# First stage of w_in: the first scale wholly on TensorE in columns of 256, x first, half of g1 on TensorE, more background loads

## The chip, the core and the metric

The kernel runs on one core of a Trainium2 chip. The metric is the device time of one execution, in microseconds. Everything is one program: matmuls on TensorE (PE), elementwise work on VectorE (DVE) and ScalarE (ACT), and nearly all loads issued by SyncE (SP) in one queue, in program order.

## The reference

Two transformer blocks on x of 256 tokens by 2048 features, in float32. The change touches the first stage of the first block and the modulation vectors around it:

```python
c_act = silu(c)                                   # 2048
mod = c_act @ w_mod[l] + b_mod[l]                 # 2048 x 12288
sh1, sc1, g1, sh2, sc2, g2 = split(mod, 6)
h = rms_norm(x, norm_attn[l]) * (1.0 + sc1) + sh1
qa, ka, va, qb, ckv, qi, ki, wi = split(h @ w_in[l])
...                                               # two attentions
x = x + g1 * (mix @ w_out[l])
h = rms_norm(x, norm_ffn[l]) * (1.0 + sc2) + sh2
x = x + g2 * conv_ffn(h, w_up[l], conv_w[l], conv_b[l], w_down[l])
```

Then follow a second block with eight more vectors of the same kind (from `c_2`), a gated MLP mixer and a latent attention. Each of the 14 vectors is a product of one row of 2048 with a matrix of 2048 by 2048, 16.8 MB of weights to load for 2048 numbers.

## The kernel before

**Layout.** Activations lie with features on partitions: `X` is 16 tiles of 128 features by 256 tokens. A weight load brings 128 by 2048 float32 (1.05 MB) into one of `NRAW` = 5 buffers with the tag `raw`, used in turn; a load waits until the one five before it is done with. `parts` (L326) splits a load into a high and a low part: ScalarE rounds (L331), VectorE subtracts (L332). `product` (L335) makes three matmuls for each pair of tiles from them (L342 to L344).

**Modulation vectors.** There are two ways to make one. `mod_part` (L431) loads 128 columns, laid out as 128 by 2048, into a `raw` buffer (tile `mraw`), and VectorE multiplies it by silu(c) and adds up, 128 results in one instruction (L452). `mod_cols` (L457) does it on TensorE: a load holds four chunks of 128 rows by 512 columns; each chunk is the moving operand of a matmul whose stationary operand is a chunk of silu(c) in the first of 32 columns, and the four write to four strips of 32 partitions of one PSUM bank. After four loads the bank is copied (L469), four small matmuls with ones add the strips and turn the line into columns (L472), and VectorE adds the bias (L474): 512 results. `sc1` has its first half by `mod_cols` and its second by `mod_part`, `g1` is by `mod_cols` whole, all others are by `mod_part`.

**Order.** `setup` (L654) interleaves the first quarter of `sc1`, four columns of `sh1`, the load of x, the squares of x (ScalarE, L676, and matmuls with ones, L678) and the reciprocal root R, which a matmul with ones spreads into a row (L299). `first_attention` (L701) then multiplies `w_a` (qi, ckv, ka, va, ki, wi: 1616 columns, 13 output tiles in 7 PSUM banks) tile by tile: `modulated` makes the modulated tile k of x, `tile_of(k)` (L717) loads tile k of `w_a` (0.83 MB), splits it and makes 39 matmuls. The vectors for later tiles are made between the tiles; `tables` (L685) loads the tables of the attention and writes a bias to DRAM that SP issues (L699) behind a small product.

Then come 16 `query` blocks with the index scores, the top-k and the first attention's heads between them, the keys and values of the second, and `w_out` in two halves of 8 blocks with the second attention's heads in the first half. The feed-forward part begins with `opening` (L363), whose first products need the shift `sh2` as two more columns (`shifts`, L532) and the scaled x of all 16 tiles.

**Background.** `mod_rest` is a generator over all vectors behind `sh1`, in the order of use (g1, sc2, sh2, g2, ...); each step issues one load and its work. `step(rate)` (L488), called with every weight block, adds the rate to a credit and takes a step for each whole one. `need(name)` (L494) runs the generator until the vector is complete, however many steps that takes:

```python
RP, RWA, RWB, RF, RG, RM = 1.0, 2.0, 1.0, 0.82, 0.5, 0.6   # L43: queries, w_out 1, w_out 2, ...

    def need(self, name):
        while name not in self.mod or self.mod[name][1] < DB:
            next(self.bg)
        return self.mod[name][0]
```

So until the feed-forward part there are 16 x 1.0 + 8 x 2.0 + 8 x 1.0 = 40 steps, of which g1, sc2 and sh2 would take 48. The framework keeps each engine's instructions in an order that a scheduler makes from the program order and priorities; SP issues in order.

Of the kernel before, what the change touches and what calls it, by code (L numbers as in the profile page):

```python
# [42 lines left out]
RP, RWA, RWB, RF, RG, RM = 1.0, 2.0, 1.0, 0.82, 0.5, 0.6  # L43
# [20 lines left out]
def _layout(a):  # L64
# [12 lines left out]
    def at(m_, a_, k_):  # L77
# [6 lines left out]
    m["w_cols"] = c(np.stack([ws[n].reshape(4, 4, P, 4, 512).transpose(3, 0, 2, 1, 4) for n in COLS])  # L84
                    ).reshape(len(COLS), 4, 4, P, 2048)
# [117 lines left out]
class Build:  # L203
# [226 lines left out]

    def mod_part(self, name, j):  # L431

        i = MODS.index(name)
        src = "c_row" if i < 6 else "c2_row"
        if self.c_src != src:
            self.c_src = src
            self.c_all = self.wp.tile([P, D], F32, name="c_all", tag="c_all", bufs=1)
            if i < 6:
                self.nc.sync.dma_start(self.c_all[:1], self.ap[src])
                for q in range(4):  # L440
                    s = slice(q * 512, q * 512 + 512)
                    ps = self.bank()
                    self.nc.tensor.matmul(ps, self.ones[:1], self.c_all[:1, s], start=True, stop=True)
                    self.nc.scalar.activation(self.c_all[:, s], ps, AF.Silu)
            else:
                self.nc.sync.dma_start(self.c_all, self.ap[src].to_broadcast((P, D)))
                self.nc.scalar.activation(self.c_all, self.c_all, AF.Silu)
# [9 lines left out]
    def mod_cols(self, name, q):  # L457
# [10 lines left out]
        line = self.pair().rearrange("p a b -> p (a b)")  # L468
        nc.scalar.copy(line, bank)  # L469
        ps = self.bank()  # L470
        for b in range(4):
            nc.tensor.matmul(ps[:, b:b + 1], line[:, b * P:(b + 1) * P], self.ones[:, :1], start=True, stop=True)  # L472
        s = slice(4 * q, 4 * q + 4)
        nc.vector.tensor_add(self.mod_tile(name)[:, s], ps[:, :4], self.vec("b_" + name, 4 * q, 4))  # L474
        self.mod[name][1] += 4
# [886 lines left out]
```

## Time and profile before

| | |
|---|---|
| time, median of 3 runs (lowest to highest) | 2346.66 us (2345.24 to 2349.06) |
| the profiled execution: its time / its span | 2345.78 us / 2344.1 us |
| TensorE matmul busy / weight load busy | 2261.0 us (96%) / 2148.6 us (92%) |
| VectorE / ScalarE busy | 1826.3 us (78%) / 1155.0 us (49%) |
| mean granted clock of TensorE | 0.984 of full speed |
| moved by the DMAs | 629.59 MB, mean 269 GB/s |
| chain that ended last, by engine | TensorE 81%, VectorE 5%, ScalarE 1%, issue 1% |

Busy times are shares of the whole span and hide the stages: the sections of the program are bound by different things. A matmul's end is modelled, so a TensorE at 10.00 of 10 us need not run at its peak. A wait is put down to what released it last. The granted clock of a stretch is 1.00 at 2.4 GHz and 0.50 at 1.2 GHz, and a mean of the two in between.

### The profile page before, as it was taken

The page shows a single profiled execution, that of the slowest core. Times are in us where ns is not written, and L with a number is a line of the kernel's source. Part 1 is how long each engine was busy: PE and PEld are TensorE (multiplying, and loading weights), DVE is VectorE, ACT ScalarE, POOL GpSimd, SP SyncE. Part 2 cuts the span into 40 slices and gives each one's busy share as a digit, 9 for nine tenths or more (in the row PEclk, how much of TensorE's full clock was granted, in tenths as well). Part 3 has the DMA queues.
Part 4 walks back from the last instruction along what each step waited for, and adds up shares of the span by engine and source line. Part 5 has one row for each costly group of instructions (what it writes and reads, how often), then busy time and mean ns, then how long its engine had stood idle before and what let it go on. Part 6 is the DMA issues. An engine that isn't in the chain of part 4 may idle for free.

```text
span 2344.1 us, 42822 instructions
## 1 busy us (share of the span) xinstructions
PE 2261.0 (96%) x17578; PEld 2148.6 (92%) x17578; DVE 1826.3 (78%) x2989; ACT 1155.0 (49%) x1926; POOL 4.9 (0%) x8
## 2 busy tenths in 40 slices
PE   6879999699999999999999999999999999899999
PEld 4777888699999999999998889999999999899899
DVE  4777478999888888888889768877776568767785
ACT  2345666465444444444566444434444356555552
POOL 0000000000000000000000000000000000000000
PEclk9899999899999999999999999999999999999999
DMA  7987698989998899898767776877776555434342
GB/s 303 364 325 252 224 337 329 337 297 348 335 371 327 317 353 345 314 359 330 277 236 259 284 282 237 312 279 272 272 270 216 180 184 185 139 143 174 140 144 90
DMA packets 98053, 629.59 MB, mean 269 GB/s; under 512 B 10977, under 2 KB 18113, under 8 KB 30785
## 3 DMA queue, kind: packets, MB, share of 16 engines
q1 hardware_dynamic: 97858, 626.87, 73.2%
q8 instruction: 137, 2.24, 0.4%
q14 instruction: 58, 0.48, 0.1%
HBM read 624.68 MB, written 2.15 MB: 267 GB/s over the span
## 4 chain that ended last, share of the span: by engine, by line
PE 81%; DVE 5%; ACT 1%; issue 1%; ACTq 0%; DVEq 0%
PE bank L342 22%; PE bank L343 22%; PE bank L344 22%; PE bank L408 4%; PE bank L409 4%; PE bank L410 4%; DVE mraw L452 1%; DVE wl L332 1%; PE bank L1048 1%; DVE X L568 0%; PE bank L1245 0%; PE bank L595 0%; ACT wh L331 0%; PE bank L390 0%; PE bank L603 0%
## 5 line engine op out<-in xcount | busy, mean ns | idle before, releaser
L342 PE MATMUL bank<-act,wh 128*128 128x256 f32 (+1 forms) x4800 | 1360.9, 284 | 22.5 <-ACT act L539 21.0
L343 PE MATMUL bank<-act,wh 128*128 128x256 f32 x4800 | 1352.7, 282 | 0.7 <-DVE act L263 0.6
L344 PE MATMUL bank<-act,wl 128*128 128x256 f32 (+1 forms) x4800 | 1350.6, 281 | 0.0
L331 ACT ACTIVATE wh<-raw 128x1024 fp32r<-128x1024 f32 (+3 forms) x770 | 764.4, 1001 | 704.2 <-PE bank L343 493.4
L332 DVE TENSOR_TENSOR wl<-raw,wh 128x1024 fp32r<-128x1024 f32 (+3 forms) x770 | 879.0, 1152 | 247.8 <-ACT wh L331 245.8
L342 PEld LDWEIGHTS bank<-act,wh 128*128 128x128 f32 x4800 | 908.3, 189 | 36.7 <-ACT act L539 21.2
L343 PEld LDWEIGHTS bank<-act,wh 128*128 128x128 f32 x4800 | 909.2, 189 | 1.7 <-DVE act L263 1.3
L344 PEld LDWEIGHTS bank<-act,wl 128*128 128x128 f32 x4800 | 907.5, 189 | 0.1
L452 DVE CUSTOM_DVE_ANT_0 mraw<-mraw,c_all,k_vecs 128x2048 f32<-128x2048 f32 x200 | 469.1, 2348 | 44.2 <-DMA mraw<-in_wmods_dram 28.3
L408 PE MATMUL bank<-wh,act 128*128 128x512 f32 (+1 forms) x392 | 152.4, 389 | 0.0
L409 PE MATMUL bank<-wl,act 128*128 128x512 f32 (+1 forms) x392 | 151.5, 386 | 0.0
L410 PE MATMUL bank<-wh,act 128*128 128x512 f32 (+1 forms) x392 | 151.3, 386 | 0.0
L262 ACT ACTIVATE act<-t 128x256 fp32r<-128x256 f32 x166 | 66.9, 414 | 112.3 <-DVE t L945 68.1
L408 PEld LDWEIGHTS bank<-wh,act 128*128 128x128 f32 x392 | 73.7, 188 | 15.9 <-PE bank L1252 1.0
L410 PEld LDWEIGHTS bank<-wh,act 128*128 128x128 f32 x392 | 73.6, 188 | 15.4 <-issue 0.7
L409 PEld LDWEIGHTS bank<-wl,act 128*128 128x128 f32 x392 | 73.7, 188 | 15.0 <-issue 0.7
L728 PE MATMUL bank<-act,wh 128*128 128x256 f32 (+1 forms) x208 | 61.0, 304 | 26.9 <-ACT wh L331 26.8
L263 DVE TENSOR_TENSOR act<-t,act 128x256 fp32r<-128x256 f32 x166 | 68.2, 424 | 17.1 <-ACT act L262 16.3
L728 PEld LDWEIGHTS bank<-act,wh 128*128 128x128 f32 (+1 forms) x208 | 41.9, 203 | 32.1 <-ACT wh L331 30.5
L934 ACT ACTIVATE t<-bank,k_vecs 128x256 f32<-128x256 f32 x41 | 23.0, 561 | 93.2 <-PE bank L344 93.2
L729 PE MATMUL bank<-act,wh 128*128 128x256 f32 (+1 forms) x208 | 59.9, 298 | 0.0
L730 PE MATMUL bank<-act,wl 128*128 128x256 f32 (+1 forms) x208 | 56.7, 304 | 0.3 <-DVE wl L332 0.3
(235 smaller groups left out, 1415.3 us busy)
## 6 DMA issues: line engine op xcount, KB each, us to landing
mraw<-in_wmods_dram SPq DMA_DIRECT2D x200, 1024.0 KB, 6.4
raw<-in_w_up_dram SPq DMA_DIRECT2D x88, 1024.0 KB, 5.9
raw<-in_w_down_dram SPq DMA_DIRECT2D x64, 704.0 KB, 5.6
raw<-in_w_u_dram SPq DMA_DIRECT2D x32, 1024.0 KB, 5.0
raw<-in_w_v_dram SPq DMA_DIRECT2D x32, 1024.0 KB, 4.9
raw<-in_w_z_dram SPq DMA_DIRECT2D x32, 1024.0 KB, 4.9
raw<-in_w_ao_dram SPq DMA_DIRECT2D x32, 1024.0 KB, 4.8
raw<-in_w_cols_dram SPq DMA_DIRECT2D x24, 1024.0 KB, 5.6
```

Of the source, the lines that this page charges most:

```text
L262: self.nc.scalar.activation(hi, src, AF.Copy)
L263: self.nc.vector.tensor_sub(lo, src, hi.bitcast(F32))
L331: nc.scalar.activation(h[:, :n], raw[:, lo:hi], AF.Copy)
L332: nc.vector.tensor_sub(l[:, :n], raw[:, lo:hi], h[:, :n].bitcast(F32))
L342: mm(ps[:, :n], h[:, s], x[:, :n], start=first and k == 0, stop=False)
L343: mm(ps[:, :T], h[:, s], x[:, LO:], start=False, stop=False)
L344: mm(ps[:, :n], l[:, s], x[:, :n], start=False, stop=last and k == len(xs) - 1)
L408: mm(ps, xh, h[:, s], start=k == 0, stop=False)
L409: mm(ps, xh, l[:, s], start=False, stop=False)
L410: mm(ps, xl, h[:, s], start=False, stop=k == kt - 1)
L452: self.nc.vector.tensor_tensor_reduce(out=raw, in0=raw, in1=self.c_all, scale=1.0, scalar=self.vec("b_" + name, j), op0=OP.mult, op1=OP.ad ...
L728: mm(ps, h[:, s], x[:, :T], start=k == 0 and i % 2 == 0, stop=False)
```

## The change

- `w_cols` is laid out in chunks of 128 rows by 256 columns, eight to a load. `mod_cols` makes 256 results from two loads: eight matmuls of 256 columns a load (two to each strip), two closing matmuls, and the line lies in a `t` tile.
- `sc1` is made by `mod_cols` whole. In `g1` the even eighths are made by two `mod_part` each and the odd ones by `mod_cols`, two loads each.
- `condition` (the silu of c, spread over partitions) is a function of its own, called first; then the loads of x and `ident`, then two loads of `sc1` and two columns of `sh1`. The squares of x are added up by VectorE (`add_square`), and two matmuls sum them (`token_sums`).
- The loop over tiles makes the vectors of the next two tiles around tile 2q and modulates them before tile 2q + 1; `tables` comes after tile 11.
- The rates: queries 1.8, `w_out` 1.25 and 1.25, which is 28 + 10 + 10 = 48 steps.

```diff
-RP, RWA, RWB, RF, RG, RM = 1.0, 2.0, 1.0, 0.82, 0.5, 0.6
+RP, RWA, RWB, RF, RG, RM = 1.8, 1.25, 1.25, 0.82, 0.5, 0.6
...
-        for i in range(4):
+        for i in range(2):
             raw = self.load(self.ap["w_cols"][COLS.index(name), q, i])
-            for e in range(4):
-                nc.tensor.matmul(bank[32 * e:32 * e + 32], self.cact[:, 4 * i + e], raw[:, e * 512:e * 512 + 512],
-                                 start=i == 0, stop=i == 3)
-            if i < 3:
+            for e in range(8):
+                r = 32 * (e % 4)
+                nc.tensor.matmul(bank[r:r + 32, :T], self.cact[:, 8 * i + e], raw[:, e * T:e * T + T],
+                                 start=i == 0 and e < 4, stop=i == 1 and e >= 4)
+            if i == 0:
                 yield
...
             if name in COLS:
-                for q in range(4):
-                    yield from self.mod_cols(name, q)
+                for q in range(8):
+                    if q % 2:
+                        yield from self.mod_cols(name, q)
+                    else:
+                        for j in (2 * q, 2 * q + 1):
+                            self.mod_part(name, j)
+                            yield
...
+        self.condition("c_row")
         a = self.mod_cols("sc1", 0)
-        for q in range(4):
+        nc.sync.dma_start(self.X, self.ap["xT"])
+        self.ident = self.load_const("ident")
+        for q in range(2):
             next(a)
             self.mod_part("sh1", q)
...
+        for k in range(DB):
+            self.add_square(self.acc, self.X[:, k], k == 0)
+        self.R = self.row(self.diagonal(self.rsqrt(self.token_sums(self.acc), 2, 1.0 / D)))
...
-            modulated(range(4))
-            a = self.mod_cols("sc1", 1)
-            for k in range(4):
-                tile_of(k)
-                next(a)
-                self.mod_part("sh1", 4 + k)
-            modulated(range(4, 8))
-            self.tables(pool)
-            done = 4
-            for k in range(8, DB):
-                self.mod_part("sc1", k)
-                self.mod_part("sh1", k)
-                modulated(range(k, k + 1))
-                for _ in range(2):
-                    if done < k:
-                        tile_of(done)
-                        done += 1
-            tile_of(DB - 1)
+            modulated(range(2))
+            for q in range(8):
+                if q < 7:
+                    a = self.mod_cols("sc1", q + 1)
+                    next(a)
+                    self.mod_part("sh1", 2 * q + 2)
+                tile_of(2 * q)
+                if q < 7:
+                    next(a)
+                    self.mod_part("sh1", 2 * q + 3)
+                    modulated(range(2 * q + 2, 2 * q + 4))
+                tile_of(2 * q + 1)
+                if q == 5:
+                    self.tables(pool)
```

The order of the instructions at three places follows. Line numbers behind L431 are shifted by a few in the changed kernel.

SP, the first loads, before and now (`raw` and `mraw` are the five buffers in turn):

```order
L240 DMA k_vecs_72<-in_vecs_dram 128x589
L323 DMA raw_82<-in_w_cols_dram 128x2048
L439 DMA c_all_88<-in_c_row_dram 1x2048
L449 DMA mraw_102<-in_wmods_dram 128x2048
L670 DMA X_79<-in_xT_dram 128x4096
L240 DMA k_ident_107<-in_ident_dram 128x128
L323 DMA raw_109<-in_w_cols_dram 128x2048
L449 DMA mraw_115<-in_wmods_dram 128x2048
L323 DMA raw_214<-in_w_cols_dram 128x2048
```

```order
L240 DMA k_vecs_72<-in_vecs_dram 128x589
L438 DMA c_all_81<-in_c_row_dram 1x2048
L677 DMA X_79<-in_xT_dram 128x4096
L240 DMA k_ident_96<-in_ident_dram 128x128
L323 DMA raw_99<-in_w_cols_dram 128x2048
L453 DMA mraw_109<-in_wmods_dram 128x2048
L323 DMA raw_113<-in_w_cols_dram 128x2048
L453 DMA mraw_130<-in_wmods_dram 128x2048
L323 DMA raw_242<-in_w_cols_dram 128x2048
L453 DMA mraw_252<-in_wmods_dram 128x2048
L323 DMA raw_255<-in_w_a_dram 128x1616
```

TensorE over the same loads, before (L678 sums the squares, L299 spreads R, L472 closes a quarter of the scale) and now (L442 spreads c, L469 and L477 are `mod_cols`, L307 sums the squares, L732 begins tile 0):

```order
L464 MATMUL bank<-raw,cact 32x512 x4
L443 MATMUL bank<-c_all,ones 128x512 x4
L678 MATMUL bank<-ones,t 128x1 x22
L464 MATMUL bank<-raw,cact 32x512 x4
L678 MATMUL bank<-ones,t 128x1 x10
L299 MATMUL bank<-t,ones 128x256
L464 MATMUL bank<-raw,cact 32x512 x8
L472 MATMUL bank<-ones,pair 128x1 x4
```

```order
L442 MATMUL bank<-c_all,ones 128x512 x4
L469 MATMUL bank<-raw,cact 32x256 x16
L477 MATMUL bank<-ones,t 128x1 x2
L307 MATMUL bank<-ones,ssacc 128x1 x2
L299 MATMUL bank<-t,ones 128x256
L469 MATMUL bank<-raw,cact 32x256 x16
L732 MATMUL bank<-act,wh 80x256
```

The load of x moved from fifth to third place, ahead of all weights. On TensorE the next scale's 16 matmuls stand behind the row of R, and tile 0 behind those.

SP, the last queries, before and now (`w_q` is a query's weight block, `bias` a head's bias, `w_uk` and `w_uv` follow the queries):

```order
L323 DMA raw<-in_w_q_dram 128x2048
L611 DMA pair<-bias 128x2x256
L323 DMA raw<-in_w_cols_dram 128x2048
L323 DMA raw<-in_w_q_dram 128x2048
L323 DMA raw<-in_w_cols_dram 128x2048
L323 DMA raw<-in_w_uk_dram 128x1024
L323 DMA raw<-in_w_uv_dram 128x2048
L323 DMA raw<-in_w_uk_dram 128x1024
```

```order
L621 DMA pair<-bias 128x2x256
L323 DMA raw<-in_w_q_dram 128x2048
L453 DMA mraw<-in_wmods_dram 128x2048 x2
L323 DMA raw<-in_w_q_dram 128x2048
L621 DMA pair<-bias 128x2x256
L453 DMA mraw<-in_wmods_dram 128x2048 x2
L323 DMA raw<-in_w_q_dram 128x2048
L453 DMA mraw<-in_wmods_dram 128x2048 x2
L323 DMA raw<-in_w_q_dram 128x2048
L453 DMA mraw<-in_wmods_dram 128x2048
L323 DMA raw<-in_w_uk_dram 128x1024
L323 DMA raw<-in_w_uv_dram 128x2048
```

Before, one background load of g1 stood between two queries; now two parts of sc2, or one, with a reduce on VectorE each.

VectorE, the end of `w_out` and the first weights of the feed-forward part, before (`raw_4687` holds the first block of `w_up`, m_sh2 is the shift) and now (`raw_4795` and `raw_4805` are the first two blocks, L578 is the residual, L538 and L317 the scaled copy and the squares):

```order
L452 ISA mraw_4659,m_sh2_4131<-mraw_4659,c_all_88,k_vecs_72 128x2048
L452 ISA m_sh2_4131 128x1
L452 ISA mraw_4662,m_sh2_4131<-mraw_4662,c_all_88,k_vecs_72 128x2048
L452 ISA m_sh2_4131 128x1
L452 ISA mraw_4665,m_sh2_4131<-mraw_4665,c_all_88,k_vecs_72 128x2048
L452 ISA m_sh2_4131 128x1
L332 TENSOR_TENSOR wl_4690<-raw_4687,wh_4689 128x1024
L537 TENSOR_TENSOR shift_4668<-m_sh2_4131,shift_4668 128x16
L332 TENSOR_TENSOR wl_4694<-raw_4687,wh_4693 128x1024
```

```order
L456 ISA mraw_4759,m_sh2_3785<-mraw_4759,c_all_81,k_vecs_72 128x2048
L456 ISA m_sh2_3785 128x1
L578 SCALAR_TENSOR_TENSOR X_79<-bank_4653,m_g1_1420,X_79 128x256
L547 TENSOR_TENSOR shift_4776<-m_sh2_3785,shift_4776 128x16
L332 TENSOR_TENSOR wl_4798<-raw_4795,wh_4797 128x1024
L538 SCALAR_TENSOR_TENSOR act_4693<-X_79,gg2_4234,act_4693 128x256
L317 TENSOR_TENSOR ssacc_80<-ssacc_80,t_4696 128x256
L578 SCALAR_TENSOR_TENSOR X_79<-bank_4701,m_g1_1420,X_79 128x256
L332 TENSOR_TENSOR wl_4802<-raw_4795,wh_4801 128x1024
L578 SCALAR_TENSOR_TENSOR X_79<-bank_4730,m_g1_1420,X_79 128x256
L538 SCALAR_TENSOR_TENSOR act_4763<-X_79,gg2_4234,act_4763 128x256
L317 TENSOR_TENSOR ssacc_80<-ssacc_80,t_4766 128x256
L332 TENSOR_TENSOR wl_4808<-raw_4805,wh_4807 128x1024
```

Before, the last residual stood 18 rows and seven reduces ahead of the shift; now the shift and the first parts of `w_up` stand between the last residuals.

## Rows read from the trace of the kernel before

**Rows 1.** TensorE's waits over the span: who waited for whom, us in total, times, longest.
```profile
PE bank L728 <- ACT wh L331: 26.8, 8, 10.2
PE bank L342 <- ACT act L539: 21.0, 1, 21.0
```
**Rows 2.** Timeline, 425 to 470 us: start, duration, engine, line, operation [idle before, releaser].
```profile
447.37 0.50 DVE L568 SCALAR_TENSOR_TENSOR X<-bank,m_g,X 128x256 f32<-128x256 f32 x1
...
447.76 2.37 DVE L452 CUSTOM_DVE_ANT_0 mraw<-mraw,c_all,k_vecs 128x2048 f32<-128x2048 f32 x1
...
462.12 2.38 DVE L452 CUSTOM_DVE_ANT_0 mraw<-mraw,c_all,k_vecs 128x2048 f32<-128x2048 f32 x1
...
465.76 1.61 ACT L539 ACTIVATE act<-shift 128x2 fp32r<-128x2 f32 x16
...
466.02 0.58 PE L342 MATMUL bank<-act,wh 128*128 128x258 f32 x1 [20.99 <-ACT act L539]
```
**Rows 3.** Timeline of SP's issues (SPq), the same stretch.
```profile
425.31 28.19 SPq L449 DMA_DIRECT2D mraw<-in_wmods_dram  x9
455.44 17.89 SPq L323 DMA_DIRECT2D raw<-in_w_up_dram  x8
```
**Rows 4.** Stages: length, busy PE, PEld, DVE, ACT, POOL, granted clock, DMA share, GB/s.
```profile
0.00:40.00 40.00, 27.32 (x98) 17.63 (x102) 8.60 (x23) 9.61 (x23) 0.20 (x4) 1.00 0.73 291
40.00:148.00 108.00, 81.78 (x585) 72.18 (x578) 84.73 (x111) 36.61 (x60) 0.00 (x0) 0.86 0.92 352
42.00:72.00 30.00, 24.32 (x183) 20.48 (x180) 19.73 (x26) 10.69 (x17) 0.00 (x0) 0.89 0.95 366
72.00:84.00 12.00, 4.83 (x30) 2.40 (x28) 8.28 (x17) 4.21 (x9) 0.00 (x0) 0.68 0.62 226
90.00:108.00 18.00, 18.00 (x141) 17.93 (x140) 16.15 (x20) 5.12 (x9) 0.00 (x0) 0.90 1.01 417
160.00:300.00 140.00, 135.21 (x1111) 112.09 (x1110) 78.64 (x229) 87.81 (x215) 0.00 (x0) 0.99 0.67 241
200.00:220.00 20.00, 20.00 (x175) 15.94 (x173) 18.95 (x83) 12.40 (x28) 0.00 (x0) 1.00 0.62 210
240.00:300.00 60.00, 59.13 (x483) 47.90 (x482) 26.25 (x67) 38.66 (x107) 0.00 (x0) 1.00 0.65 227
330.00:390.00 60.00, 59.87 (x492) 51.91 (x491) 56.66 (x117) 42.98 (x121) 0.00 (x0) 1.00 0.96 357
430.00:440.00 10.00, 10.00 (x87) 10.00 (x87) 10.00 (x18) 4.89 (x11) 0.00 (x0) 1.00 0.84 300
```
**Rows 5.** Timeline of the first stage, several engines, lines left out between them.
```profile
32.38 0.16 DVE L271 TENSOR_SCALAR rs_x<-bank 128x2 f32<-128x2 f32 x1 [13.63 <-PE bank L678]
...
37.50 1.22 PE L299 MATMUL bank<-t,ones 128*128 128x256 f32 x2 [5.16 <-DVE t L293]
...
48.78 0.50 PE L728 MATMUL bank<-act,wh 128*80 128x256 f32 x1 [4.72 <-ACT wh L331]
...
78.40 0.31 SPq L699 DMA_DIRECT2D bias<-pT  x1
...
87.96 0.58 PE L728 MATMUL bank<-act,wh 128*128 128x256 f32 x1 [10.17 <-ACT wh L331]
...
143.41 0.60 ACT L519 ACTIVATE t<-t,m_sh,gg 128x256 f32<-128x256 f32 x1 [6.15 <-DVE m_sh L452]
...
152.00 0.60 ACT L519 ACTIVATE t<-t,m_sh,gg 128x256 f32<-128x256 f32 x1 [6.15 <-DVE m_sh L452]
...
160.38 0.37 ACT L754 COPY pair<-bank 64x256 f32<-64x256 f32 x1 [3.46 <-PE bank L730]
```
**Rows 6.** Groups: xcount | busy us, mean ns | idle before; TensorE 160 to 310, VectorE 0 to 466.
```profile
L464 PE MATMUL bank<-raw,cact 128*32 128x512 f32 x128 | 17.0, 605 | 0.0
L472 PE MATMUL bank<-ones,pair 128*128 128x1 f32 x32 | 4.2, 253 | 3.2 <-ACT pair L469 3.2
L452 DVE CUSTOM_DVE_ANT_0 mraw<-mraw,c_all,k_vecs 128x2048 f32<-128x2048 f32 x56 | 131.1, 2350 | 21.8 <-ACT c_all L444 14.7 <-DMA mraw<-in_wmods_dram 7.2
```

More of the change, by code (lines that the diff above doesn't have):

```diff
@@ L83, in _layout @@
     ws, bs = at(wm, wa, wk), at(bm, ba, bk)
[L84 to L85 removed]
+    m["w_cols"] = c(np.stack([ws[n].reshape(2, 8, P, 8, T).transpose(3, 0, 2, 1, 4) for n in COLS])
+                    ).reshape(len(COLS), 8, 2, P, 2048)
     m["wmods"] = c(np.stack([ws[n].reshape(D, DB, P).transpose(1, 2, 0) for n in MODS]))
@@ L429, in mod_tile, with condition @@
         return self.mod[name][0]
+    def condition(self, src):
+        if self.c_src == src:
+            return
+        self.c_src = src
+        self.c_all = self.wp.tile([P, D], F32, name="c_all", tag="c_all", bufs=1)
+        if src == "c_row":
+            self.nc.sync.dma_start(self.c_all[:1], self.ap[src])
+            for q in range(4):
+                s = slice(q * 512, q * 512 + 512)
+                ps = self.bank()
+                self.nc.tensor.matmul(ps, self.ones[:1], self.c_all[:1, s], start=True, stop=True)
+                self.nc.scalar.activation(self.c_all[:, s], ps, AF.Silu)
+        else:
+            self.nc.sync.dma_start(self.c_all, self.ap[src].to_broadcast((P, D)))
+            self.nc.scalar.activation(self.c_all, self.c_all, AF.Silu)
     def mod_part(self, name, j):
         i = MODS.index(name)
[L434 to L439, printed above, removed]
-                for q in range(4):
[L441 to L447, printed above, removed]
+        self.condition("c_row" if i < 6 else "c2_row")
         raw = self.wp.tile([P, D], F32, name="mraw", tag="raw", bufs=NRAW)
@@ L664, in setup @@
         self.acc = self.con.tile([P, T], F32, name="ssacc")
+        self.condition("c_row")
         a = self.mod_cols("sc1", 0)
-        for q in range(4):
+        nc.sync.dma_start(self.X, self.ap["xT"])
+        self.ident = self.load_const("ident")
+        for q in range(2):
             next(a)
             self.mod_part("sh1", q)
-            if q == 0:
-                nc.sync.dma_start(self.X, self.ap["xT"])
-                self.ident = self.load_const("ident")
-            if q == 1:
-                ss = self.bank()
-                for k in range(DB):
-                    sq = self.tmp()
-                    nc.scalar.activation(sq, self.X[:, k], AF.Square)
-                    for tb in range(2):
-                        nc.tensor.matmul(ss[:, tb:tb + 1], sq[:, tb * P:(tb + 1) * P], self.ones[:, :1],
-                                         start=k == 0 and tb == 0, stop=k == DB - 1 and tb == 1)
-                self.R = self.row(self.diagonal(self.rsqrt(ss[:, :2], 2, 1.0 / D)))
+        for k in range(DB):
+            self.add_square(self.acc, self.X[:, k], k == 0)
+        self.R = self.row(self.diagonal(self.rsqrt(self.token_sums(self.acc), 2, 1.0 / D)))
         self.bg = self.mod_rest()
```

13 lines of the change are left out of this document (7 added, 6 removed).

## Prediction

> **What bounds the kernel now.** I read the page's chain of waits first: TensorE carries most of it, and its busy time is 96% of the span, so time can be won only where TensorE stands. The next view is therefore TensorE's own waits [rows 1]. Two of them hold nearly everything: 21.0 us in one piece in front of `product` (L342), and 26.8 us in eight pieces in front of the `w_a` tiles (L728).
>
> The large one lies where the feed-forward part begins. VectorE runs the reduces of `sh2` (L452) one behind the other, seven of them from 447.76 to 464.5 us; ScalarE spreads the shift made of them (L539), and only then TensorE starts, after 20.99 us of idling [rows 2]. The queue shows why: nine background loads go out in a row, from 425.31 on, and the first load of `w_up` follows at 455.44 [rows 3]. It is `need("sh2")`, which finds 8 of 16 columns done, since the 40 credits of the three earlier stages buy only 16 (g1), 16 (sc2) and 8 columns.
>
> The stages [rows 4]: from 160 to 300 us, the sixteen queries, TensorE is busy for 135.21 of 140 us while VectorE has 78.64 us of work and the DMAs move 241 GB/s: there is room beside TensorE. In 330 to 390 us, the first half of `w_out`, VectorE is at 56.66 of 60, the DMAs at 0.96 and 357 GB/s, and TensorE still at 59.87. Up to 148 us the loads bind: 352 GB/s from 40 to 148, with 226 in the hole from 72 to 84.
>
> **The change, part by part.** All sums are made against the profiled execution, 2345.78 us; the median of the runs shown is 0.9 us above it.
>
> *1. The burst in front of the feed-forward part.* 16 queries at 1.8, 8 blocks at 1.25 and 8 at 1.25 give 48 steps, which are exactly g1, sc2 and sh2. `need("sh2")` then loads nothing. In VectorE's new order the shift stands ahead of the last two residual updates of `w_out`, and the parts of the first `w_up` blocks between those; so the first product can follow the last product of `w_out`. Eight reduces at 2350 ns [rows 6] are 18.8 us of the 20.99. What stays is at most the tail of the last residual (0.50 us for X [rows 2], and about as much for each half of its scaled copy), about 1.5 us. I take -19.5 us; ends -15 (VectorE arrives late by two reduces) and -20.5.
>
> *2. `w_out`.* The first half has 10 background steps instead of 16, the second 10 instead of 8. The first half runs at TensorE's rate already (330 to 390 us) [rows 4], so fewer reduces give nothing I would count. In the second half VectorE is full (10.00 of 10 from 430 to 440, TensorE 10.00 as well [rows 4]), and two more reduces are 4.7 us on it; a part of that reaches TensorE. I take +1.5; ends -2 and +5.
>
> *3. The queries.* TensorE loses 8 of its 16 blocks of g1. Sixteen took 17.0 us, 1.06 each [rows 6]. A block's eight matmuls of 256 columns move as many columns as four of 512 did. Lower bound 1.06 again; upper bound 2.12, if each group of four costs what a group of 512 columns costs. I take 1.2, near the lower end, because the four of a group run side by side in the row. The four closing groups (L472, 4.2 us and 3.2 us of idling) have half the matmuls: -2.1. Together 17.0 - 8 x 1.2 + 2.1 = 9.5 us off TensorE; with 2.12 it is 2.1, with 1.06 10.6.
> The Trainium skill, TensorEngine Tiling (Array Packing), section Instruction Overhead, speaks against the halving: about 60 cycles for each matmul whatever its width. By it the four more matmuls of a block would cost some 0.1 us (an estimate at 2.4 GHz), and the term would be about 9.8 instead of 9.5. No row here has the 256-column form.
> What is added hides beside TensorE or not at all: 20 reduces (8 of g1, 12 of sc2), 20 x 2350 ns = 47.0 us, on a VectorE that had 78.64 of 140 us. That is 125.6 us in the 130.5 that TensorE needs, 96%; the stretch 330 to 390 kept TensorE fed at 94%. It is uneven: between 200 and 220 us, where the top-k runs, VectorE already has 18.95 of 20 us, and four parts fall there (9 us); from 240 to 300 it has 26.25 of 60, and 12 parts (28 us) still fit. The queue moves 16 loads of `w_q`, 28 background loads of 1.05 MB and 8 of 0.26, 48.2 MB; in 130.5 us that is 370 GB/s, against 357 and 417 in rows 4. All loads go through SP in order and through five raw buffers, so a late reduce holds back the `w_q` load behind it. I give back 5.5 us: -4 in all, ends -10.6 (cover complete) and +8.
>
> *4. The first stage.* X comes ahead of the big loads, but R, the reciprocal roots as a row, hardly comes sooner. Before, the root starts at 32.38 and R's matmul runs at 37.50 [rows 5]. Now the squares are added up by VectorE, 15 adds, in an order that puts three reduces and one half of a weight tile among them; each reduce waits for its load, so I place R at 37 to 38 us again. TensorE reaches the next scale's matmuls only behind R, and the fifth raw buffer is freed there: the loads halt at about 11.6 MB near 32 us and go on at 39 (estimates from the rate of 90 to 108 us [rows 4] and 2 us to land). Before, 11.6 MB (40 us x 291 GB/s) were also in at 40 us. So the DMAs have gained nothing there, although the first tile starts at about 41 instead of 48.78, since the scale no longer waits for a fourth load.
> From 40 us 38 MB remain in both. Before, they took 108 us at 352 GB/s: the hole from the tables (SP waits for L699 until 78.40, and TensorE idles 10.17 us, to 87.96), and then VectorE's pace, 8.6 us for a tile with two reduces and one weight split (143.41 to 152.00) [rows 5]. Now a tile has one reduce of 2.35 us fewer on VectorE, so the loads bind again: 2.93 MB a tile. I take 378 GB/s, between 366 for the same mixture of loads (42 to 72 us) and 417: 100.5 us. `tables` comes later; its wait on SP is bounded by one tile on TensorE, and I put 3 us in. With 2 us for landing the last tile is in at 145.5 us. Behind it three tiles stand on TensorE in a row (the last scale is finished ahead of them): 39 matmuls each at 18 us / 141 [rows 4] are 5.0 us, of which some 10 us lie behind the last load, and the sums are read 1 us later, at 156.5 instead of 160.38. So -4; ends -16 (417 GB/s, no wait) and +4 (352).
> Part 4 frees and fills the same raw buffers as before; the work moved from VectorE to TensorE (8 blocks of sc1) has cover as long as TensorE waits for loads.
>
> Sum: -19.5 + 1.5 - 4 - 4 = -26 us; 2345.8 - 26 = 2319.8 for the profiled execution, 2321 for a median.
>
> **Rivals.**
> *A. The queries become bound by loads or VectorE.* For it: 370 GB/s and 96% are asked at once, and VectorE is nearly full from 200 to 220. Against it: 330 to 390 us. Price: 48.2 MB at 350 GB/s are 137.7 us instead of 130.5, 7.2 back; if the four top-k queries also give back one reduce each, 9.4 us, the two make +7 out of the -9.5. Part 3 is then about 0 to +8, and the time 2325 to 2333, more with 2 us of waits behind it.
> The Trainium skill, DMA: Bandwidth & Descriptors, section Bandwidth, sets some 358 GB/s as what HBM gives one core; 48.2 MB would then take 134.6 us (an estimate), which is inside this rival. The stretch 90 to 108 us, with 417 GB/s, speaks against that limit here.
> *B. The first stage gains more:* the loads run at 417 GB/s and the tables' wait is covered. Part 4 is then -16 and the time 2309.
> *C. Slower.* One mechanism: in the queries every second load is now a part whose buffer is freed by VectorE, in order behind the attention's work, and not by TensorE. If each of the 16 queries waits for one whole reduce (2.35 us), that is 37.6 us, part 3 is -9.5 + 37.6 = +28, the sum -22 + 28 = +6, and the time 2353. It decides from 2.0 us a query on, where 16 x 2.0 eat up the 31.5 us of everything else. Against it: five buffers hold nearly two queries' loads, and in 330 to 390, where two parts stood to one weight load, TensorE did not wait.
> *D. The change doesn't do what it says.* The 256-column blocks cost 2.12 (7.4 us lost over the queries' eight, more in the first stage, where waits cover it), and VectorE's backlog at the end of `w_out` keeps half of the 21 us. Part 1 is then -10, part 3 +3, and the time 2338; with the backlog whole, 2346.
>
> **How the numbers follow.** Forecast (2311 to 2326) 0.57; A (2326 to 2336) 0.18; B (below 2311) 0.12; D 0.07; C 0.06. Predicted 2321. From 2304 to 2337 the range takes in the forecast, A, and most of B; what is left out is C, most of D and the far end of B, 0.17 or so. About 0.2%, 4.7 us, is what a measurement of this kernel can tell from no change: faster by more 0.88, within it 0.05 (the slow half of D, C at its mildest), slower by more 0.07.
>
> **What would show it.** Part 1: TensorE's longest wait is no longer L342 behind the shift, no row of SP holds nine background loads in a row, and the gap before the first `w_up` product is under 3 us. Part 3: the stretch from the first `w_q` product to `w_uk` shortens by about 4 us, with VectorE above 90% and the DMAs near 370 GB/s; a wait of L342 to L344 for `wl` or `wh` behind a `w_q` load would be A, or C if it is longer than the gain. The group of L469 shows the price of a 256-column block. Part 4: first tile near 41 us, tiles 7.5 to 8 us apart, sums read near 156 us. The forecast is wrong if the first stage ends after 164 us, if the queries take longer than before, or if a new wait of 10 us stands anywhere behind 470 us, where the order is the old one and only moves forward.

## The result, and the profile after

The changed kernel takes 2310.16 us (median of 4 runs, 2308.47 to 2315.10) where the kernel before takes 2345.95 (4 runs, 2345.05 to 2349.06): a ratio of 0.9849, 95% interval 0.9830 to 0.9867. That is 35.8 us less where 25 were forecast; the time lies inside the range, 11 us below the number predicted. The profiled execution of the changed kernel is the longest of its four, 2315.1 us with a span of 2311.9 (the span runs from the first instruction to the last); against the profile before, the span is 32.2 us shorter.

Five events on TensorE part the span into six stages: the first product of the queries, the last, the first of `w_out`, the first of its second half, and the first of the feed-forward part. First the kernel before, then the changed one, with the columns of [rows 4] (length, busy TensorE, weight loads, VectorE, ScalarE, GpSimd, granted clock, DMA share, GB/s):

```profile
0.00:166.63 166.63, 124.60 (x792) 103.87 (x793) 103.88 (x145) 57.20 (x102) 0.20 (x4) 0.90 0.86 332
166.63:315.22 148.59, 143.41 (x1170) 120.48 (x1167) 85.44 (x238) 86.49 (x211) 0.00 (x0) 0.98 0.70 250
315.22:329.31 14.09, 14.09 (x95) 11.49 (x93) 13.04 (x27) 10.36 (x28) 0.00 (x0) 1.00 1.01 402
329.31:403.90 74.59, 74.45 (x591) 65.26 (x589) 67.00 (x135) 50.30 (x138) 0.00 (x0) 1.00 0.90 335
403.90:466.02 62.12, 41.13 (x323) 40.08 (x321) 61.72 (x86) 24.25 (x46) 0.00 (x0) 0.86 0.90 332
466.02:2344.07 1878.05, 1863.31 (x14620) 1807.43 (x14620) 1495.22 (x2363) 926.38 (x1405) 4.68 (x4) 1.00 0.71 259
```

```profile
0.00:154.76 154.76, 117.89 (x932) 95.46 (x933) 97.12 (x152) 59.89 (x108) 0.20 (x4) 0.97 0.92 362
154.76:300.99 146.23, 136.24 (x1161) 120.66 (x1160) 120.91 (x272) 85.19 (x211) 0.00 (x0) 0.95 0.86 316
300.99:315.04 14.05, 14.05 (x95) 11.44 (x93) 10.19 (x26) 9.26 (x26) 0.00 (x0) 1.00 0.97 387
315.04:388.69 73.65, 73.65 (x591) 64.88 (x589) 64.99 (x129) 53.45 (x143) 0.00 (x0) 1.00 0.88 323
388.69:429.79 41.10, 41.10 (x322) 40.25 (x321) 41.10 (x65) 23.50 (x55) 0.00 (x0) 1.00 0.90 331
429.79:2311.90 1882.11, 1865.77 (x14622) 1810.29 (x14620) 1495.14 (x2368) 929.02 (x1394) 5.69 (x4) 1.00 0.71 257
```

Row by row the lengths differ by -11.9, -2.4, 0.0, -0.9, -21.0 and +4.1 us, together -32.2. So the first stage and the fifth row, where the burst of background loads stood, carry the gain, the queries give little, and the last row, where the code is the same, is 4 us longer in this execution.

TensorE's waits over the span answer to [rows 1]; the wait for the shift is gone and L732 (then L728) has 4.1 us instead of 26.8:

```profile
PE bank L307 <- DVE ssacc L317: 13.1, 1, 13.1
PE bank L477 <- ACT t L474: 9.2, 10, 2.2
PE bank L732 <- ACT wh L331: 4.1, 7, 1.5
```

Timelines of TensorE and SP where the feed-forward part begins, against [rows 2, 3]: the product with 258 columns follows the last one of `w_out` without a pause, and one background load stands in front of six loads of `w_up`, where nine stood:

```profile
429.67 0.29 PE L344 MATMUL bank<-act,wl 128*128 128x256 f32 x1
429.79 0.29 PE L342 MATMUL bank<-act,wh 128*128 128x258 f32 x1
```
```profile
407.68 0.33 SPq L453 DMA_DIRECT2D mraw<-in_wmods_dram  x1
411.08 19.68 SPq L323 DMA_DIRECT2D raw<-in_w_up_dram  x6
```

The first stage against [rows 5]: the sums of squares, the row R, the first tile, the write of the bias, and the first sums read.

```profile
34.67 1.01 PE L307 MATMUL bank<-ones,ssacc 128*128 128x1 f32 x4 [13.09 <-DVE ssacc L317]
...
38.61 1.22 PE L299 MATMUL bank<-t,ones 128*128 128x256 f32 x2 [2.93 <-DVE t L293]
...
42.98 0.46 PE L732 MATMUL bank<-act,wh 128*80 128x256 f32 x2
...
125.39 0.32 SPq L703 DMA_DIRECT2D bias<-pT  x1
...
148.71 0.37 ACT L754 COPY pair<-bank 64x256 f32<-64x256 f32 x1 [0.82 <-PE bank L734]
```

R came at 38.6 us, close to the 37 to 38 predicted and 1.1 us later than before; the first tile came 5.8 us sooner than before; the sums 11.7 us sooner, at 148.7 and not at 156.5.

### The profile page after: what moved, and what is told of

Read it like the earlier page. It is cut to its first block, busy times and chain, and to the rows that moved or that the text cites. A ratio compares the mean times of both kernels' runs of the same rounds, so it can differ in the third digit from the quotient of the medians.

```text
span 2311.9 us, 43143 instructions
## 1 busy us (share of the span) xinstructions
PE 2248.7 (97%) x17710; PEld 2143.0 (93%) x17710; DVE 1829.5 (79%) x3008; ACT 1160.3 (50%) x1932; POOL 5.9 (0%) x8
## 4 chain that ended last, share of the span: by engine, by line
PE 88%; DVE 5%; DMA 3%; ACT 2%; issue 1%; SPq 0%; DVEq 0%; ACTq 0%
PE bank L342 23%; PE bank L343 23%; PE bank L344 23%; PE bank L408 4%; PE bank L409 4%; PE bank L410 4%; DVE wl L332 2%; DMA mraw<-in_wmods_dram 1%; DVE mraw L456 1%; PE bank L734 1%; ACT wh L331 1%; PE bank L732 1%; DMA raw<-in_w_a_dram 1%; PE bank L733 1%; PE bank L469 1%
## 5 line engine op out<-in xcount | busy, mean ns | idle before, releaser
L732 PE MATMUL bank<-act,wh 128*128 128x256 f32 (+1 forms) x208 | 58.2, 295 | 4.2 <-ACT wh L331 4.1
L578 DVE SCALAR_TENSOR_TENSOR X<-bank,m_g,X 128x256 f32<-128x256 f32 x96 | 46.0, 479 | 5.6 <-PE bank L344 4.3
```

What stands on the lines that cost most here:

```text
L732: mm(ps, h[:, s], x[:, :T], start=k == 0 and i % 2 == 0, stop=False)
```

## The experiments

Medians in us, with the ratio to the kernel before and its 95% interval. Each ratio is to runs of the kernel before from the same series, whose medians lie between 2344.2 and 2347.9 us; between series, compare the ratios.

| kernel | median | ratio |
|---|---|---|
| changed kernel | 2310.2 | 0.9849 (0.9830 to 0.9867) |
| e1: kernel before, new rates | 2320.3 | 0.9888 (0.9874 to 0.9903) |
| e2: changed, old rates | 2322.0 | 0.9898 (0.9883 to 0.9913) |
| e3: half of the scale by reduces | 2312.2 | 0.9851 (0.9833 to 0.9869) |
| e4: bias written later | 2306.8 | 0.9832 (0.9819 to 0.9845) |
| e5: second scale ahead of R | 2312.0 | 0.9855 (0.9841 to 0.9868) |
| e6: closing one step later | 2304.8 | 0.9827 (0.9812 to 0.9841) |
| e7: closing behind the next load | 2304.9 | 0.9828 (0.9814 to 0.9841) |
| e8: squares summed on TensorE | 2316.8 | 0.9886 (0.9870 to 0.9902) |
| e9: x loaded later | 2312.5 | 0.9865 (0.9849 to 0.9882) |
| v1: e4 + e5 + e7 | 2303.5 | 0.9819 (0.9805 to 0.9832) |
| v2: e4 + e7, rates 1.8, 2.0, 0.5 | 2309.2 | 0.9850 (0.9835 to 0.9865) |
| v4: v1, no step with the last block | 2301.2 | 0.9800 (0.9787 to 0.9814) |

### The rates alone, and the rest alone (e1, e2)

```diff
-RP, RWA, RWB, RF, RG, RM = 1.0, 2.0, 1.0, 0.82, 0.5, 0.6
+RP, RWA, RWB, RF, RG, RM = 1.8, 1.25, 1.25, 0.82, 0.5, 0.6
```

e1 is this edit on the kernel before, e2 its reverse on the changed kernel.

> The kernel before with nothing but the three rates changed (1.8, 1.25, 1.25); g1 stays wholly on TensorE and the first stage is the old one. Theory: the 21.0 us that TensorE idled in front of the first product of the feed-forward part go whole, the second half of w_out is no longer for its 10 background steps, and the 12 reduces that come into the queries find room beside TensorE, so that the queries change by less than 1 us: 2324 to 2327 us. Rival (the 5.5 us that my prediction gave back for a full VectorE and full queues): the queries, which now carry 28 background loads of 1.05 MB beside 16 weight loads, get longer by 4 to 7 us: 2329 to 2332.

> The changed kernel with the old rates (1.0, 2.0, 1.0). The queries then hold exactly g1, 8 loads for TensorE and 8 for VectorE, instead of 28 background loads. Theory: the 7 us missing from the 8.4 that TensorE saves on the blocks of g1 are waits of TensorE for a copy on ScalarE (6.2 us in four pieces in front of the closing matmuls, 3.6 in front of a transpose), which more or fewer reduces on VectorE do not touch; so only the stall of 21 us comes back: 2330 to 2333 us. Rival: VectorE and the loads of the 12 further columns cost the queries those 5 to 7 us; then they get shorter here, and the time is 2324 to 2327.

Queries and second half of `w_out` of e1, then of e2:

```profile
165.91:311.94 146.03, 140.91 (x1170) 119.14 (x1167) 107.19 (x259) 86.86 (x211) 0.00 (x0) 0.99 0.85 321
...
401.29:442.39 41.10, 41.10 (x323) 40.25 (x321) 41.00 (x65) 24.80 (x57) 0.00 (x0) 1.00 0.91 341
```
```profile
154.17:290.01 135.84, 130.08 (x1161) 115.34 (x1160) 98.74 (x251) 85.26 (x211) 0.00 (x0) 1.00 0.73 263
...
379.91:441.12 61.21, 41.32 (x323) 40.26 (x321) 60.20 (x86) 24.35 (x46) 0.00 (x0) 0.86 0.89 334
```

The burst's price is shown: with the new rates alone 62.1 us become 41.1, and with the old ones they are 61.2 again. e1 came out below both expectations: 12 further reduces cost its queries nothing (148.6 to 146.0 us). e2 came out 2 us below its rival: without those 12 columns the changed kernel's queries take 135.8 us and not 146.2. So the theory fell that the background load doesn't matter there, but only for the changed kernel: with the new blocks of g1 the queries are 10.4 us longer when the 12 loads are there, with the old ones they are not. The two gains, 26.3 us (e1) and 24.6 (e2), each against the runs of the kernel before in the same series, don't add: together they are 35.8.

### What the queries lose (e6, e7)

TensorE's waits in the changed kernel's queries, and the stretches with a lowered granted clock in them (between the two levels, 1.2 and 2.4 GHz):

```profile
PE bank L477 <- ACT t L474: 6.2, 4, 2.2
PE bank L605 <- ACT s L648: 3.6, 1, 3.6
PE bank L807 <- ACT pair L765: 1.4, 1, 1.4
```
```profile
175.00:180.00 5.00, 5.00 (x32) 5.00 (x31) 4.14 (x4) 1.06 (x1) 0.00 (x0) 0.66 0.98 362
230.00:235.00 5.00, 2.97 (x37) 2.15 (x28) 4.63 (x16) 4.31 (x11) 0.00 (x0) 0.87 0.99 382
235.00:240.00 5.00, 5.00 (x36) 5.00 (x36) 4.57 (x5) 3.38 (x13) 0.00 (x0) 0.79 1.00 409
275.00:280.00 5.00, 2.07 (x7) 1.22 (x8) 2.31 (x3) 2.51 (x6) 0.00 (x0) 0.81 1.04 397
280.00:285.00 5.00, 5.00 (x20) 3.45 (x19) 4.55 (x5) 2.13 (x4) 0.00 (x0) 0.51 0.47 180
```

The two closing matmuls of an eighth of g1 (L477) stand in TensorE's queue right behind the last block, and wait until ScalarE, which has weight parts and softmax rows in front of it, has copied the bank (L474). In two of the cases, and behind the wait for L648, a stretch with a lowered clock follows; a wait of 2.2 us ends at 173.69, and the clock is at 0.66 from 175 to 180. The mean over the queries is 0.95 against 1.00 in e2. In the changed kernel's queries TensorE is idle for 10.0 us against 5.8 in e2, and busy for 136.2 us against 130.1 with the same 1161 matmul records: together the 10.4.

e6 puts a step of the background between the copy and the closing; e7 keeps the closing back until the next weight load (`step` first runs what is open):

```diff
         line = self.tmp()
         nc.scalar.copy(line, bank[:, :T])
+        if name != "sc1":
+            yield
...
```
```diff
...
     def step(self, rate):
+        while self.open:
+            self.open.pop()()
...
```

> The changed kernel with the two closing matmuls of an eighth of g1 one background step later, so that TensorE no longer stands in front of them while ScalarE copies the bank. Theory: TensorE's 6.2 us of waiting in the four closing groups of the queries go, and TensorE is what the queries wait for: 4 to 6 us less, 2304 to 2306 us. Rival: the queries are held by VectorE or the loads anyway, and the wait moves to another line: 2309 to 2311.

> The changed kernel with the closing matmuls of an eighth of g1 behind the next query's weight load, so that all four of them stand behind a whole product; the one-step delay left two of four in place, since at a rate of 1.8 two steps often fall together. Theory: TensorE's four waits for ScalarE's copy go, 6.2 us, and with the two long ones (2.2 and 2.0 us) the lowered granted clock that follows them (0.66 from 175 to 180 us, 0.87 and 0.79 from 230 to 240: 5 x 0.34 + 5 x 0.13 + 5 x 0.21 = 3.4 us): 2300 to 2303 us. Rival: a wait and the clock behind it come back at the next place, and it stays where one step of delay was: 2304 to 2306.

e7's queries, and its one wait of TensorE in the second half of `w_out`:

```profile
152.91:289.35 136.44, 132.86 (x1160) 117.69 (x1160) 117.99 (x269) 81.91 (x208) 0.00 (x0) 0.99 0.90 336
```
```profile
PE bank L342 <- ACT act L560: 2.6, 1, 2.6
```

With all 28 background loads at 336 GB/s and VectorE at 86% (117.99 of 136.44), e7's queries take about what e2's take with 16. So neither the queue nor VectorE was full. But not all of the 9.8 us hangs on where the four small pairs of matmuls stand. The 3.6 us in front of L605 went too, though nothing was edited there, and all but 0.6 us of them went in e3 (below), which leaves the closings where they were:

```profile
PE bank L477 <- ACT t L474: 5.1, 4, 1.5
...
PE bank L605 <- ACT s L648: 0.6, 1, 0.6
```

e3's queries took 140.4 us. The five profiled kernels with the long wait for L648 and the closings in place (the changed one, e4, e5, e8, e9) took 144.1 to 147.0 in the queries, the five with the closings moved (e6, e7, v1, v2, v4) 136.4 to 139.0. So the moved closings are worth some 4 us (140.4 against 136.4), and the rest goes with the wait in front of L605; why that wait comes and goes was not tried.

e7's median is 5.3 us below the changed kernel's, the time that its rival gave. In the traces the two lie 10.5 us apart, but the changed kernel's is of its longest run; and in e7 TensorE waits 2.6 us for the shift again (second half 44.1 us, not 41.1), since VectorE makes both of the last residuals, behind a reduce of `sh2`, before the shift. The same order, wait and length stand in e6, and also in e3, whose closings are where they were; what brings this order is open. e6 has two of the four waits left, 138.9 us, and the same time.

### The first stage (e3, e4, e5, e8, e9)

e3 makes the second half of `sc1` by `mod_part` again, two reduces a tile.

```diff
-                if q < 7:
-                    a = self.mod_cols("sc1", q + 1)
-                    next(a)
+                if q < 3:
...
+                elif q < 7:
+                    self.mod_part("sc1", 2 * q + 2)
...
```

> The changed kernel with the second half of the first scale again as reduces on VectorE, in the new order of tiles; the bytes loaded are the same. Theory: tiles 7 to 13 become VectorE's again, 8.6 us apart as before instead of the 7.4 us that the loads give, about 8 to 10 us more in the first stage: 2317 to 2321 us. Rival: the loads set the pace either way (VectorE has work for 72 of 108 us from 40 to 148 us, and for 19 us more with these eight reduces), so nothing changes beyond 2 us: 2309 to 2312.

```profile
0.00:158.37 158.37, 112.18 (x788) 94.19 (x789) 114.15 (x164) 59.23 (x104) 0.20 (x4) 0.94 0.90 356
158.37:298.78 140.41, 132.55 (x1160) 118.82 (x1160) 118.02 (x269) 82.67 (x208) 0.00 (x0) 0.98 0.87 322
```

The stage is 3.6 us longer, between the two expectations, and the time is the same: its queries were 5.8 us shorter, with 0.6 us of waiting in front of L605, and its second half of `w_out` 3.0 us longer. So the scale's second half on TensorE is worth little in the stage, and nothing that can be measured in the time.

e4 takes the write of the bias out of `tables` and issues it behind `tile_of(13)`.

```diff
...
                 if q == 5:
-                    self.tables(pool)
+                    bt = self.tables(pool)
+                if q == 6:
+                    nc.sync.dma_start(self.bias, bt)
```

> The changed kernel with the write of the attention's bias issued two tiles later than the product it waits for, so that SP has no reason to stand there; everything else of the tables stays. Theory: the loads set the pace of the first stage, and the only hole left in them after 44 us is the one at the tables, 259 GB/s from 124 to 132 us where 400 flow beside it, 2.8 us of loads: 2306.5 to 2308.5 us. Rival: TensorE's three last tiles behind the loads, or the start of the queries, take it back: 2309 to 2311.

The stretch 124 to 132 us, in the changed kernel and in e4:

```profile
124.00:132.00 8.00, 6.32 (x41) 4.47 (x41) 4.64 (x5) 1.65 (x2) 0.00 (x0) 0.79 0.70 259
```
```profile
124.00:132.00 8.00, 6.05 (x48) 3.95 (x47) 4.76 (x6) 1.64 (x2) 0.00 (x0) 1.00 1.01 417
```

The hole fills up, the stage ends 2.8 us sooner (151.93), and the median falls by 3.3, the size that the theory has; the intervals of the two ratios overlap. That the filled hole made the gain is not shown: with the changed kernel's first stage e2, e6 and e7 ended it at 154.2, 153.6 and 152.9 us, with e4's edit in it v2 and v4 ended it at 153.2 and 154.7, and 3.7 us of e4's shorter span lie behind the start of the feed-forward part.

e5 puts the first load of the second eighth, with its matmuls, ahead of the sums; e8 sums the squares by 32 small matmuls as before the change; e9 loads x behind two weight loads.

```diff
+        self.a1 = self.mod_cols("sc1", 1)
+        next(self.a1)
         for k in range(DB):
             self.add_square(self.acc, self.X[:, k], k == 0)
...
```
```diff
-            self.add_square(self.acc, self.X[:, k], k == 0)
+            nc.scalar.activation(sq, self.X[:, k], AF.Square)
+            for tb in range(2):
+                nc.tensor.matmul(ss[:, tb:tb + 1], sq[:, tb * P:(tb + 1) * P], self.ones[:, :1],
...
```
```diff
-        nc.sync.dma_start(self.X, self.ap["xT"])
...
         for q in range(2):
             next(a)
             self.mod_part("sh1", q)
+            if q == 0:
+                nc.sync.dma_start(self.X, self.ap["xT"])
...
```

> The changed kernel with the first load of the second eighth of the scale, and its eight matmuls, ahead of the sums of squares on TensorE and not behind the row of R, so that its buffer comes free before TensorE's wait of 13.1 us. Theory: it is this buffer that halts the loads between 30 and 44 us (207 GB/s from 30 to 40, 163 from 36 to 44, 400 beside it); its 4 to 5 us come off the end of the first stage: 2305 to 2307 us. Rival: the buffers behind it wait for VectorE's reduces and for the row of R as well, so the halt only moves by one load: 2309 to 2311.

> The changed kernel with the squares of x summed on TensorE again, as before the change, with x still loaded first. Theory: what puts R at 38.6 us now is VectorE, which has 15 adds and three reduces between 20 and 40 us (16.5 of 20 us busy) while TensorE waits 13.1 us; without the adds R comes 3 to 5 us sooner, the loads' halt from 35 to 42 us ends sooner by as much, and since loads set the pace behind it, the first stage ends 3 to 5 us sooner: 2305 to 2307 us. Rival: R waits for the reduce in front of the root's last steps and for TensorE's 32 small matmuls (9.6 us before), so nothing is gained, or 1 to 2 us lost: 2309 to 2312.

> The changed kernel with x loaded where it was before, behind one load of the scale and one of the shift. Theory: those 2.1 MB are 5 us of loads at 420 GB/s; the squares start 5 us later, R comes 3 to 5 us later, the loads halt longer, and the first stage ends 3 to 5 us later: 2313 to 2315 us. Rival (what my prediction said: R stays near 38 us with x first or not, because VectorE's reduces stand in front of the adds either way): within 1.5 us, 2309 to 2312.

The halt of the loads and the stretch behind it, in the changed kernel and in e5; then e8's squares and its row R:

```profile
30.00:44.00 14.00, 6.40 (x47) 3.83 (x47) 12.68 (x30) 3.90 (x8) 0.00 (x0) 1.00 0.49 166
44.00:60.00 16.00, 16.00 (x150) 14.39 (x148) 10.38 (x14) 4.62 (x9) 0.00 (x0) 1.00 1.00 398
```
```profile
30.00:44.00 14.00, 6.32 (x32) 4.20 (x33) 12.89 (x32) 4.84 (x9) 0.00 (x0) 1.00 0.92 350
44.00:60.00 16.00, 16.00 (x145) 14.70 (x143) 9.39 (x13) 3.95 (x7) 0.00 (x0) 1.00 0.73 276
```
```profile
20.71 13.79 PE L687 MATMUL bank<-ones,t 128*128 128x1 f32 x64
39.71 1.22 PE L299 MATMUL bank<-t,ones 128*128 128x256 f32 x2 [5.21 <-DVE t L293]
```

e5's edit fills the halt (2.6 MB more from 30 to 44 us) and opens another behind it (2.0 MB less from 44 to 60): the halt moves, as its rival has it, and the time is the rival's to 1 us. Its stage ends at 151.99, 0.9 us before that of e7, whose first stage is unedited. In e8 the theory fell outright, and the time lies above its rival's too: TensorE needs 13.8 us for the small matmuls (14.0 in the kernel before, in two pieces of 9.6 and 4.4; the rival counted the first alone), R comes 1.1 us later, the stage ends 3.7 us later, and the time is 6.7 us longer (4.3 longer than e9's in the same series). VectorE's adds, which look like the bottleneck in front of R, are the cheaper way. In e9 R comes at 38.8 us with x later, and the stage ends at 153.6: the rival, which is the prediction's own step, holds for R. The time, 2312.5, lies between the two expectations.

### Together (v1, v2, v4)

v1 is e4, e5 and e7; v2 leaves e5 out and changes the rates; v4 is v1 with

```diff
-            for e, ps in enumerate(self.half_blocks(ap["w_out"][1, j], mix_b, rate, pairs if j in WOB else None)):
+            for e, ps in enumerate(self.half_blocks(ap["w_out"][1, j], mix_b, rate if j < 7 else 0, pairs if j in WOB else None)):
```

and a rate of 1.32 there, so that the last block has no step.

> The last three edits together (bias written later, second scale ahead of the sums, closings behind the next weight load). Theory: three different waits, so the gains add: 2.8 + 4 + 9 us off 2310: 2293 to 2298 us. Rival: what the first stage ends earlier, the queries lose again, since their loads (1.05 MB x 44) then start with less lead: 2300 to 2303.

> Bias written later and closings behind the next weight load, with the rates 1.8, 2.0 and 0.5: 28, 16 and 4 steps, and none with the last block of w_out. With the closings moved, VectorE had a reduce of sh2 in front of the last two residuals of w_out, TensorE waited 2.6 us for the shift again, and the second half of w_out took 44.1 us instead of 41.1. Theory: that wait is the order on VectorE alone; with the 12th to 16th reduce of the first half taken there (TensorE kept its rate beside 16 of them before) the second half takes 41.1 us again, 3 us off what the two edits gave: 2298 to 2301 us. Rival: 16 reduces in the first half cost TensorE 2 us there (74.6 and 75.9 us with 16, 73.6 with 10), and the sum stays at 2301 to 2304.

> The three edits together (bias written later, second scale ahead of the sums, closings behind the next weight load), the 10 steps of w_out's second half at 1.32 over its first seven blocks and none with the last, so that VectorE has no reduce of sh2 in front of the last two residuals; the first half keeps its 10 steps, since 16 cost TensorE 6 us there. Theory: the 2.6 us of waiting for the shift go and the second half takes 41.1 us again instead of 44.1, with nothing else touched: 3 us off 2303.5, 2299 to 2302 us. Rival: VectorE is full in that half, and the same reduce one block earlier delays the residuals all the same: 2302 to 2305.

v1's gains don't add to what was expected: its queries keep e7's gain (136.8 us), its first stage ends 3.3 us sooner and not 6.8 (v4, with the same first stage, ended it at 154.7 us, no sooner than the changed kernel), and the wait of 2.6 us for the shift is in it as in e7. v2 came out above both of its expectations: its first half of `w_out`, with 16 reduces, took 79.59 us instead of 73.65, where the kernel before and e2 took 74.6 and 75.9 with as many; why it is longer here is open. v4 shows the wait in the second half in another place, in front of a weight part. The first half of v2, then v4's wait:

```profile
304.05:383.64 79.59, 76.51 (x590) 65.61 (x589) 69.93 (x139) 50.70 (x135) 0.00 (x0) 1.00 0.91 340
```
```profile
PE bank L344 <- DVE wl L332: 2.6, 1, 2.6
```

So v4's median is what its theory said, but not by it: its second half took 45.6 us in the trace, and the rival is right about the place. v4 has the lowest median here, 9.0 us below the changed kernel, with intervals that don't meet; v1's interval overlaps with v4's.

## Why the prediction was right, and by how much each step was off

| step | predicted (ends) | measured in the traces |
|---|---|---|
| 1. burst | -19.5 (-20.5 to -15) | -21.0 |
| 2. `w_out` | +1.5 (-2 to +5) | -0.9 |
| 3. queries | -4 (-10.6 to +8) | -2.4 |
| 4. first stage | -4 (-16 to +4) | -11.9 |
| behind the feed-forward part's start | 0 | +4.1 |

The mechanisms of steps 1 and 2 were right, and step 4 went the way forecast; that the sum came so near is in part luck. The forecast's own band was 2311 to 2326; the measured 2310.16 lies just below it, in the band of rival B (0.12), whose rate of 417 GB/s didn't come. Step 4 gained 7.9 us more than its term, and 4.1 us that no term held took half of that back in the traces.

**1 and 2.** The mechanism was right: 48 steps for 48 do away with the whole wait, in e1 too, where nothing but the rates is new. I kept 1.5 us for "the tail of the last residual"; there is none (429.79, no idle time). And VectorE, "full in the second half", costs TensorE nothing there: 41.13 us of TensorE's work before, 41.10 now. That it is close is seen in e3, e6 and e7, where another order at the end makes 3 us.

**3.** The sum came out nearly right, by luck, with two terms wrong in it. A block of 256-column matmuls was taken at 1.2 us, between 1.06 and 2.12. The groups of the queries, against [rows 6]:

```profile
L469 PE MATMUL bank<-raw,cact 128*32 128x256 f32 x128 | 8.2, 384 | 0.0
L477 PE MATMUL bank<-ones,t 128*128 128x1 f32 x16 | 2.6, 264 | 6.2 <-ACT t L474 6.2
```

Eight blocks (a block is eight matmuls, 16 records) took 8.2 us, 1.03 each: halving the width cost nothing, and rival D is out (its own sum, -10 + 1.5 + 3 - 4, gives 2336, or 2337 for a median, and not 2338). The Trainium skill, TensorEngine Tiling (Array Packing), section Instruction Overhead, has some 60 cycles for each matmul; twice as many matmuls show none of it here (1.03 us against 1.06), so the measurement decides against adding it.
The closing groups were the term that failed: I took 2.1 us off because they have half the matmuls. There are still four of them, each waits for one copy, and with their waiting they went from 7.4 us [rows 6] to 8.8. The Trainium skill names this in TensorEngine Tiling (Array Packing), section PSUM Bottleneck: packing speeds TensorE up, not the emptying of its banks, which may then bind. The trace agrees only in part: TensorE waited up to 2.2 us for one copy, but the copy itself took 0.39 us, and ScalarE had other work in front of it.
The 5.5 us given back were put on VectorE at 96% and the queue at 370 GB/s. VectorE was at 83% (120.91 of 146.23) and the queue at 316 GB/s, so two signs that the prediction named for this step, VectorE above 90% and near 370 GB/s, did not come, and e7 at 336 GB/s and 86% was 9.8 us shorter. What was given back, 10 us against e2, is waits for ScalarE and TensorE's longer busy time at the lowered clock; which of the waits carry how much is shown only as far as e3 and e7 part them. Rival A named the right stage and the wrong cause; C (a whole reduce for each query) does not show.

**4.** This step was right in its direction and wrong in its size: -11.9 against -4, most of what was under-called. I put the loads' halt "at about 11.6 MB near 32 us". In the trace, 40 us at 339 GB/s are 13.6 MB, and the halt is from 35 to 42. The reason is in SP's and VectorE's timelines:

```profile
31.77 0.33 SPq L323 DMA_DIRECT2D raw<-in_w_a_dram  x1
35.32 0.33 SPq L323 DMA_DIRECT2D raw<-in_w_cols_dram  x1
```
```profile
29.39 2.35 DVE L456 CUSTOM_DVE_ANT_0 mraw<-mraw,c_all,k_vecs 128x2048 f32<-128x2048 f32 x1
...
34.53 0.77 DVE L332 TENSOR_TENSOR wl<-raw,wh 128x592 fp32r<-128x592 f32 x1
```

The second load of `w_a` goes out at 31.77, when a reduce ends, and the next at 35.32, when the first tile of `w_a` is split. The load five before that of 31.77 is still in its buffer then: its matmuls run at 39.76. So the buffers aren't taken strictly in turn, as I had it here and in the section on the kernel before; a load takes one that is free. 2 MB more are 5.1 us at 392 GB/s. The rest is the rate; I took 378 GB/s between 366 and 417:

```profile
44.00:116.00 72.00, 66.60 (x595) 58.29 (x597) 48.14 (x67) 24.54 (x43) 0.00 (x0) 0.98 0.99 392
```

28.2 MB at 392 instead of 378 are 2.7 us. The two make 7.8, as much as the distance from 156.5 to 148.71. This is a sum over the trace; no kernel was run with the buffers in turn. The 3 us for the tables' wait were right (259 GB/s for 8 us where 400 flow beside it, an estimated 2.8 us of loads), as was R's place (e9), and what the prediction didn't ask, whether TensorE's half of the scale matters behind the loads, e3 answers with 3.6 us. Rival B had the right sign, at a rate that the stage as a whole doesn't reach.

**Behind the start of the feed-forward part** nothing new waits, as predicted, but the changed kernel's profile is 4.1 us longer there than the one before. That is no accident of one execution: e5, e8 and e9 take 1881.0 to 1882.2 us there as well, and the other ten kernels, with the same code and rates, 1876.2 to 1880.2. What sets it was not tried.

## What to carry to other kernels

Look for what stands *behind* a small dependent operation in an in-order queue: four pairs of one-column matmuls made TensorE stand for 6.2 us until another engine had copied, beside 8.2 us for the eight blocks that they closed, and behind two of them the clock fell. Issuing such a closing one unit of work later took these waits away. When gains lie in different stages, measure each alone and both: here 26.3 and 24.6 us made 35.8, and the difference was waits for ScalarE and the clock behind them. Before an edit gets the credit for a stage, look at the same stage in every kernel whose code is the same there: e3 shortened the queries by 5.8 us without an edit in them. And before you time a halt of loads, ask which buffer each load takes.

## What the runs showed of the hardware

- In the queries, 1.03 us for eight matmuls of 256 columns on 32-column strips, 1.06 for four of 512: no price for the width.
- The loads of one core ran at 392 GB/s over 72 us and at 417 over 8 us (e4), above the some 358 GB/s that the Trainium skill (DMA: Bandwidth & Descriptors, section Bandwidth) has as the limit of HBM for one core; the measurement decides.
- Behind waits of 2.0 to 3.6 us the granted clock was 0.51 to 0.87 for stretches of 5 us; e2 had waits of up to 2.0 us and a clock of 1.00 throughout its queries.
- With the granted clock at 1.00 and TensorE without a wait, the trace has 2537 or 2538 matmul records over 720 to 920 and 1000 to 1100 us in the changed kernel, e5, e8 and e9, and 2546 to 2551 in the other ten kernels. That is some 0.4% in the same code, in the four kernels that are also the slowest behind the start of the feed-forward part; it isn't explained.
